# Attention in a latent-attention layer: probabilities times values by four query blocks, and where the rotary queries are made

## The chip, the cores and the metric

One NeuronCore of a Trainium2 chip runs the whole kernel. The metric is device time in microseconds (us) from launch to end. The engines work side by side, each through its own queue in order: TensorE (PE) multiplies matrices into PSUM, VectorE (DVE) and ScalarE (ACT) read PSUM and write SBUF, GpSimd (POOL) works on SBUF alone, and SyncE (SP) issues most of the DMAs.

## What is computed

One layer of a streaming encoder: 1024 tokens, width 1024, 16 heads (cut to what matters; `norm` is the RMS norm):

```python
u = norm(x, g) @ w_in                       # c_q 384 | c_kv 256 | k_rope 32 | z 1024
q = (norm(c_q) @ w_q_b)                     # per head 64 plain + 32 rotary columns
kv = norm(c_kv) @ w_kv_b                    # per head k_nope 64, v 64
q_rope, k_rope = rope(q[..., 64:]), rope(k_rope)
s = (q_nope @ k_nope.T + q_rope @ k_rope.T) * scale   # per block of 128 queries,
p = softmax(where(k_chunk <= q_chunk, s, -inf))       # keys up to the block's end, chunks of 64
x = x + (concat(p @ v) * silu(z)) @ w_out
x = x + sigmoid(norm(x) @ ple_gate) * (p_i @ ple_proj)
return norm(x, final_norm)
```

## The kernel before

All of it is in float32, in which each operand of a product is split into a high part, rounded to the PE's fast float32 form, and the low rest; a product is three matmuls (high times high, high times low, low times high). The program has five stages: u (the 672 columns of c_q, c_kv and k_rope, about 5 to 62 us of the trace), z (eight feature blocks `c`, to 161 us), attention (to about 507 us), the output projection, and the gate.

In **z**, each block `c` is 48 matmuls of 512 columns (L513). Its weights come in two halves through `z_weights`: SP loads `zs` (one buffer), ACT scales it to `zh` (L360), DVE makes the rest `zl` (L361); the halves are asked for two ahead. DVE scales the block on its way out of PSUM (L516).

**Rotary queries** are made by `project_r(g, hf)` for four heads `g` and one half `hf` of the tokens: nine matmuls of 512 columns (L423), two DVE products with the cosine and sine tables `cs` into the tile `rt` (L435), an ACT copy of the high part into `rh` (L438), a POOL subtraction that leaves the low part in `rt` (L91), and two POOL DMAs that write `rh` and `rt` to DRAM (L441), from where `rope_q` loads single heads. `rt` and `rh` have one buffer each, so a new `rt` can be written only when the DMA that reads the one before has landed. Before, two of the eight calls stand in z (blocks 4 and 5) and six among the heads 2, 6 and 10 of attention.

In **attention**, heads run one after the other, and in each head the eight blocks of 128 queries in the order of the list `ORDER`. For a block: scores on PE (`scores`, L609), maximum on DVE (L614), exponential on ACT (L619); two blocks later PE transposes the probabilities 128 by 128 (L121), ACT copies the high part of P^T (L650) and DVE the low part; when both blocks of a pair are there, `values` multiplies P^T by the values (L661), and o is evicted and multiplied with z. `project_k` makes the keys of two heads: DVE copies one head's rows to `kst` (L556) and makes `k_lo` of the other. Products take PSUM banks from a ring of four (`ps_pj`, `ps_o`, `ps_tr`), scores from two larger ones. A scheduler orders the instructions on each engine.

Line numbers are those of the kernel before, unless a fence says otherwise. The functions that the change touches follow.

Of the kernel before, what the change touches and what calls it, by code (L numbers as in the profile page):

```python
# [9 lines left out]
F32 = mybir.dt.float32  # L10
# [7 lines left out]
P = 128  # L18
S = 1024
# [17 lines left out]
ORDER = (5, 4, 2, 3, 7, 6, 0, 1)  # L37
# [3 lines left out]
V_AT, K_AT, Q_AT, R_AT = (4, 4, 2, 2), (0, 3), (6, 7), (1, 6)  # L41
# [10 lines left out]
def mla_ple_kernel(ctx, tc, x, x_t, p_t, pos, norm_g, w_c, w_z, q_norm, w_q, w_r, kv_norm, w_k, w_v,  # L52
# [9 lines left out]
    def pool(name, bufs=1, **kw):  # L62
        return tc.tile_pool(name=name, bufs=bufs, **kw)
# [327 lines left out]
    cs = [att1.tile([P, S], F32, name=f"cs{e}") for e in range(2)]  # L391
# [3 lines left out]
    def load_split(src, cols, name, bufs):  # L395
# [3 lines left out]
        hi = att1.tile([P, n], F32R, tag=name + "h", name=name + "h", bufs=bufs)  # L399
        lo = att1.tile([P, n], F32R, tag=name + "l", name=name + "l", bufs=bufs)  # L400
# [26 lines left out]
    def project_r(g, hf):  # L427
# [4 lines left out]
        ps = product_q(wr_of[g], hf)  # L432
# [68 lines left out]
    zw = zph.enter_context(pool("zw", reuse_waits="tile"))  # L501

    for c in range(KT):
# [20 lines left out]
        if c == 3:  # L524
            weights(0)
        if c in (4, 5):
            project_r(0, c - 4)
# [8 lines left out]
    pt_w = [[att.tile([P, n, 2 * P], F32R, name=f"pt{n}{z}") for z in "hl"] for n in (4, 8)]  # L536
    for n, w in zip((4, 8), pt_w):
        for z in w:
            G.memset(z[:, n - 1, :P].bitcast(F32), 0.0)
    pt = [[z[:, (2, 0, 2, 0)[g]:, :] for z in pt_w[g // 2]] for g in range(4)]  # L540
    vals = att.tile([P, NT, 2, 4, VD], F32R, name="vals")
    kst = att.tile([P, S], F32, name="kst")
# [4 lines left out]
    def project_k(c, hf):  # L547
# [93 lines left out]
    def prob_transposes(h, i, pr):  # L641
        g = i // 2
        hi, lo = pt[g]
        half = slice(0, P) if i % 2 == 0 else slice(P, 2 * P)
        for j0 in range(0, i + 1, 4):
# [4 lines left out]
            A.copy(out=hi[:, j0:j0 + n, half], in_=src)  # L650
            sub_hi(V, lo[:, j0:j0 + n, half], src, hi[:, j0:j0 + n, half])

    def values(h, g):
        e, c = h % 2, h // 2
        hi, lo = pt[g]
        ps = ps_o()
        last = 2 * g + 1
# [5 lines left out]
        o = att.tile([P, 256], F32, tag="o1", name="o1", bufs=2)  # L663
        A.copy(out=o[top], in_=ps[bot, :256])
        V.tensor_tensor(out=o[top], in0=ps[top, :256], in1=o[top], op=ALU.add)  # L665
        z = zT[top, c, g * 256:(g + 1) * 256]
# [18 lines left out]
    for n in range(len(blocks) + LAGV):  # L685
        if n < len(blocks):
# [209 lines left out]
```

## Time and profile before

| | us |
|---|---|
| median of three runs (719.19 to 720.9) | 719.9 |
| the profiled execution | 719.65 |
| its span, first to last instruction | 717.9 |
| PE busy in the span | 703.2 (98%) |
| DVE, ACT, POOL busy | 523.8, 400.5, 214.2 |

Matmuls overlap in this trace: a record lasts longer than the distance to the next one's start. What PE can do is read from distances of starts, not from durations. The profiled execution took 719.65 us, 1.75 us more than its span, for launch and end.

### The profile page before, as it was taken

To read this page: it belongs to the slowest core of one execution; us is meant where nothing else is said; L and a number is where in the kernel's file an instruction comes from. 1 tells how busy PE (TensorE), PEld (TensorE's weight loads), DVE (VectorE), ACT (ScalarE), POOL (GpSimd) and SP (SyncE) were. 2 spreads that over 40 slices of the span, in tenths; PEclk is the share of its full clock that TensorE was granted. 3 is DMA by queue.
4 is the path that set the end of the run, shared out by engine and by line. 5 is a ranking of instruction groups with operands and counts; after the bars stand their busy time and mean duration, and the time that the engine had idled before them with its cause. 6 is when DMAs were issued, how large, how long until landed. Compare 5 with 4: busy or idle time off the path is not lost.

```text
span 717.9 us, 11582 instructions
## 1 busy us (share of the span) xinstructions
PE 703.2 (98%) x4032; PEld 612.9 (85%) x4032; DVE 523.8 (73%) x1298; ACT 400.5 (56%) x920; POOL 214.2 (30%) x236
## 2 busy tenths in 40 slices
PE   9999999999999999999999999989999999999995
PEld 7999888888988899889988899878878888888884
DVE  6995553417888888888888888899564168888754
ACT  6752343417777767877767787776353145342322
POOL 0000443214145434554335532264155142000000
PEclk9999999999999999999999999999999999999999
DMA  8720334314103402052211421032573030111101
GB/s 318 279 89 12 122 100 125 103 60 110 38 16 108 147 31 74 1 181 74 66 40 60 136 60 60 15 108 85 179 265 115 1 102 24 38 37 37 60 30 59
DMA packets 26907, 63.95 MB, mean 89 GB/s; under 512 B 4568, under 2 KB 8544, under 8 KB 26848
## 3 DMA queue, kind: packets, MB, share of 16 engines
q1 hardware_dynamic: 23168, 52.19, 22.8%
q0 software_dynamic: 3536, 11.02, 4.6%
q8 instruction: 32, 0.52, 0.3%
q14 instruction: 27, 0.22, 0.1%
q10 hardware_dynamic: 144, 0.00, 0.0%
HBM read 50.01 MB, written 13.18 MB: 88 GB/s over the span
## 4 chain that ended last, share of the span: by engine, by line
PE 90%; DVE 3%; ACT 3%; DMA 2%; issue 1%; POOL 0%; SPq 0%; ACTq 0%; DVEq 0%
PE ps_big L751 21%; PE ps_big L609 13%; PE ps_big L513 12%; PE ps_o L661 10%; PE ps_tr L121 9%; PE ps_pj L423 6%; PE ps_big L215 4%; PE ps_pj L751 3%; PE ps_pj L570 3%; PE ps_pj L553 3%; PE ps_big L216 3%; PE ps_o L215 1%; PE ps_pj L216 1%; DMA wst<-in_w_out 1%; ACT prob L619 1%; PE ps_tr L609 1%
## 5 line engine op out<-in xcount | busy, mean ns | idle before, releaser
L751 PE MATMUL ps_big<-w,aTh 128*128 128x512 f32 (+1 forms) x480 | 139.0, 390 | 0.0
L751 PEld LDWEIGHTS ps_big<-w,aTh 128*128 128x128 f32 x480 | 89.4, 188 | 20.2
L619 ACT ACTIVATE prob<-ps_big,mx 128x384 f32<-128x384 f32 (+6 forms) x112 | 89.4, 798 | 16.2 <-DVE mx L614 15.5
L614 DVE TENSOR_REDUCE mx<-ps_big 128x1 f32<-128x384 f32 (+6 forms) x112 | 91.6, 818 | 1.8
L121 PE MATMUL ps_tr<-ident,prob 128*128 128x128 f32 x576 | 84.1, 273 | 2.0 <-ACT prob L619 2.0
L751 PE MATMUL ps_big<-w,aTl 128*128 128x512 f32 (+1 forms) x240 | 84.6, 390 | 0.0
L121 PEld LDWEIGHTS ps_tr<-ident,prob 128*128 128x128 f32 x576 | 68.3, 140 | 11.7 <-ACT prob L619 2.8
L91 DVE TENSOR_TENSOR pt8l<-ps_tr,pt8h 128x512 fp32r<-128x512 f32 (+3 forms) x128 | 71.0, 582 | 4.5 <-ACT pt8h L650 3.8
L667 POOL TENSOR_TENSOR zT<-o,zT 64x256 f32<-64x256 f32 x56 | 41.1, 736 | 94.2 <-DVE o L665 80.6
L609 PE MATMUL ps_big<-k_hi,qh 128*128 128x512 f32 (+2 forms) x176 | 67.7, 385 | 0.9 <-ACT prob L619 0.8
L650 ACT CAST pt8h<-ps_tr 128x512 fp32r<-128x512 f32 (+3 forms) x128 | 60.7, 509 | 4.7 <-PE ps_tr L121 4.3
L609 PE MATMUL ps_big<-k_lo,qh 128*128 128x512 f32 (+2 forms) x176 | 62.0, 352 | 0.0
L609 PE MATMUL ps_big<-k_hi,ql 128*128 128x512 f32 (+2 forms) x176 | 61.4, 349 | 0.0
L661 PE MATMUL ps_o<-pt8h,vals 128*128 128x256 f32 x224 | 57.6, 294 | 0.0
L661 PE MATMUL ps_o<-pt8l,vals 128*128 128x256 f32 x224 | 55.0, 282 | 0.0
L751 PEld LDWEIGHTS ps_big<-w,aTl 128*128 128x128 f32 x240 | 45.0, 188 | 10.2 <-POOL aTl L91 0.5
L116 ACT ACTIVATE jk<-xs 128x512 bf16<-128x512 f32 (+2 forms) x25 | 18.8, 751 | 45.2 <-DVE xs L829 37.3
L661 PEld LDWEIGHTS ps_o<-pt8l,vals 128*128 128x128 f32 x224 | 42.9, 191 | 0.0
L661 PEld LDWEIGHTS ps_o<-pt8h,vals 128*128 128x128 f32 x224 | 42.6, 190 | 0.0
L650 ACT CAST pt4h<-ps_tr 128x384 fp32r<-128x384 f32 (+3 forms) x64 | 27.2, 426 | 27.3 <-PE ps_tr L121 27.1
L360 ACT ACTIVATE zh<-zs,g_col 128x128 fp32r<-128x128 f32 x56 | 18.3, 392 | 42.1 <-DMA zs<-in_w_z 36.1
L609 PEld LDWEIGHTS ps_big<-k_hi,qh 128*128 128x128 f32 x176 | 33.2, 189 | 7.7 <-ACT prob L619 3.5
(285 smaller groups left out, 1740.2 us busy)
## 6 DMA issues: line engine op xcount, KB each, us to landing
zT<-in_x SPq DMA_DIRECT2D x8, 512.0 KB, 5.0
rlb<-rl SPq DMA_DIRECT2D x32, 128.0 KB, 3.1
wst<-in_w_out SPq DMA_DIRECT2D x8, 512.0 KB, 4.4
xs<-in_x SPq DMA_DIRECT2D x8, 512.0 KB, 7.2
wst<-in_ple_gate SPq DMA_DIRECT2D x8, 512.0 KB, 4.0
out<-xs SPq DMA_DIRECT2D x16, 256.0 KB, 2.0
zs<-in_w_z SPq DMA_DIRECT2D x14, 256.0 KB, 2.9
zT<-in_x_t SPq DMA_DIRECT2D x6, 512.0 KB, 4.1
```

The costliest lines, as they stand in the source:

```text
L91: eng.tensor_tensor(out=lo, in0=src, in1=hi.bitcast(F32), op=ALU.subtract)
L121: nc.tensor.transpose(dst[:, j * P:(j + 1) * P], src[:, j * P:(j + 1) * P], ident)
L215: nc.tensor.matmul(pq, st, mv[:, k, :QL], start=first, stop=last)
L423: nc.tensor.matmul(ps, w[b][:, k, :], (cq_hi, cq_lo)[a][:, k, hf * 512:hf * 512 + 512], start=k == 0 and a + b == 0, stop=k == n - 1 and a ...
L513: nc.tensor.matmul(ps[:, hf * 512:(hf + 1) * 512], wz[b][:, k % 4, :], (hT_hi, hT_lo)[a][:, k, hf * 512:(hf + 1) * 512], start=k == 0 and ...
L609: nc.tensor.matmul(ps[:, off + s0:off + s1], q[a][:, qs], (k_hi, k_lo)[b][e][:, s0:s1], start=a + b == 0, stop=a == 1)
L614: V.tensor_reduce(out=mx, in_=s, axis=AX.X, op=ALU.max, negate=True)
L619: A.activation(out=pr[:, :n], in_=s, func=AF.Exp, bias=mx, scale=1.0, accum_out=l)
L650: A.copy(out=hi[:, j0:j0 + n, half], in_=src)
L661: nc.tensor.matmul(ps[:, :256], w, z[:, j, :], start=j + n == 0, stop=j == last and n == 1)
L667: (V if h >= H - 2 else G).tensor_tensor(out=z, in0=o[top], in1=z, op=ALU.mult)
L751: nc.tensor.matmul(o, st[a][:, k, :], w[k][b][:, cols], start=k == 0 and a + b == 0, stop=k == nk - 1 and a == 1)
```

## The change

1. `ORDER` becomes (5, 4, 1, 0, 7, 6, 3, 2). `values` runs for four query blocks at once (`g = i // 4`): up to 512 columns in one matmul. P^T is packed: below the diagonal four blocks side by side, on the diagonal four, three, two and one (10 blocks of 128 columns in all), so the diagonal's matmuls have 512, 384, 256 and 128 columns. Each diagonal group of four transposes is copied in two parts (three and one). The evictions of o have 512 columns instead of 256.
2. All eight `project_r` calls stand in z: two after each of the blocks 4 to 7, with their weights (`weights_r`) loaded one group ahead; `cs` moves to a pool that ends with z. None is left in attention.
3. `kst`, a tile of its own before, is now the tile `rt`.
4. `rsqrt` makes its first guess in one DVE instruction instead of two, and its Newton step with one column uses `scalar_tensor_tensor` in place of `tensor_scalar`.
5. The last token block's final scaling goes out in four pieces of 256 columns (two on ACT, two on DVE), one of them through ACT's own DMA queue.

```diff
-ORDER = (5, 4, 2, 3, 7, 6, 0, 1)
+ORDER = (5, 4, 1, 0, 7, 6, 3, 2)
...
-        half = small.tile([P, n], I32, tag=f"rs_i{n}", name="rs_i", bufs=2)
-        V.tensor_scalar(out=half, in0=v.bitcast(I32), scalar1=1, scalar2=None,
-                        op0=ALU.logical_shift_right)
-        V.tensor_scalar(out=y.bitcast(I32), in0=half, scalar1=-1, scalar2=0x5F3759DF,
+        V.tensor_scalar(out=y.bitcast(I32), in0=v.bitcast(I32), scalar1=-0.5, scalar2=0x5F3759DF,
...
-                V.tensor_scalar(out=t, in0=y, scalar1=y, scalar2=h, op0=ALU.mult, op1=ALU.mult)
+                V.scalar_tensor_tensor(out=t, in0=y, scalar=y, in1=h, op0=ALU.mult, op1=ALU.mult)
...
-        if c == 3:
-            weights(0)
-        if c in (4, 5):
-            project_r(0, c - 4)
+            wr = weights_r(0)
+        if c >= 4:
+            for hf in range(2):
+                project_r(c - 4, wr, hf)
+            if c + 1 < KT:
+                wr = weights_r(c - 3)
+            else:
+                weights(0)
...
-    kst = att.tile([P, S], F32, name="kst")
+    kst = {}
...
+        if hf == 0:
+            kst[0] = rt_tile("kst")
+        V.tensor_copy(out=kst[0][NOPE:, cols], in_=ps[NOPE:])
...
+            if j0 < 4 * g:
+                parts = [(slice(0, 4), slice(q, 16, 4))]
+            else:
+                m = min(n, 3)
+                parts = [(slice(0, m), slice(16 * g + q, 16 * g + q + 3 * m - 2, 3))]
+                if n == 4:
+                    parts.append((slice(3, 4), slice(16 * g + 7, 16 * g + 8)))
...
-        for j in range(last + 1):
-            w = vals[:, j, c % 2, 2 * e:2 * e + 2, :]
-            for n, z in enumerate((hi, lo)):
-                nc.tensor.matmul(ps[:, :256], w, z[:, j, :], start=j + n == 0, stop=j == last and n == 1)
+        steps = [(j, n) for j in range(4 * g + 4) for n in range(2)]
+        steps.append(steps.pop(1))
+        for j, n in steps:
+            q = max(j - 4 * g, 0)
+            at = 4 * j if j < 4 * g else 16 * g + (7 if q == 3 else 4 * q)
+            nc.tensor.matmul(ps[:, q * P:], vals[:, j, c % 2, 2 * e:2 * e + 2, :],
+                             pt[g][n][:, at:at + 4 - q, :], start=j + n == 0, stop=(j, n) == (0, 1))
...
-                if h % 4 == 2 and h + 2 < H and at in R_AT:
-                    project_r(h // 4 + 1, R_AT.index(at))
...
-        for hf in range(2):
-            cols = halves[hf]
-            if last and hf == 0:
+        for i, cols in enumerate([slice(z, z + 256) for z in range(0, D, 256)] if last else halves):
+            on_act = last and i < 2
+            if on_act:
```

Three places show what the scheduler makes of it. On DVE, the end of z and the start of attention before: `rt` is written by the last rotary product of z, then come the scaling of the last z blocks and the first keys and queries (a bracket lists what an instruction waits for: DMAHW and DMASW are DMAs of SP's and of POOL's queue).

```order
L435 TENSOR_TENSOR rt_1587<-ps_pj_1577,cs0_982 128x512 [waits DMASW5_49,PE_49,Pool_49]
L435 TENSOR_TENSOR rt_1587<-ps_pj_1577,cs1_983 128x512
...
L516 TENSOR_TENSOR zT_81<-ps_big_1595,rbc_994 128x1024 [waits PE_49]
L516 TENSOR_TENSOR zT_81<-ps_big_1670,rbc_994 128x1024 [waits PE_49]
L556 COPY kst_1736<-ps_pj_1750 64x512 [waits DVE_49,Activation_49]
L91 TENSOR_TENSOR k_lo0_988<-ps_pj_1750,k_hi0_987 64x512
```

The same place on DVE with the change:

```order
L515 TENSOR_TENSOR zT_81<-ps_big_1609,rbc_974 128x1024 [waits PE_49]
L429 TENSOR_TENSOR rt_1696<-ps_pj_1686,cs0_987 128x512 [waits DMASW3_49,PE_49,Pool_49]
L429 TENSOR_TENSOR rt_1696<-ps_pj_1686,cs1_988 128x512
L429 TENSOR_TENSOR rt_1714<-ps_pj_1704,cs0_987 128x512 [waits DMASW5_49,PE_49,Pool_49]
...
L515 TENSOR_TENSOR zT_81<-ps_big_1728,rbc_974 128x1024 [waits PE_49]
L429 TENSOR_TENSOR rt_1791<-ps_pj_1781,cs0_987 128x512 [waits DMASW7_49,PE_49,Pool_49]
...
L429 TENSOR_TENSOR rt_1809<-ps_pj_1799,cs0_987 128x512 [waits DMASW1_49,PE_49,Pool_49]
...
L557 COPY kst_1867<-ps_pj_1859 64x512 [waits DMASW3_49,Pool_49]
L91 TENSOR_TENSOR k_lo0_968<-ps_pj_1859,k_hi0_967 64x512
```

The last four rotary products (of eight, from block 4 on) stand here, each behind the landing of a POOL DMA, and the first copy to `kst`, ahead of every `k_lo`, waits for the last of them.

On SP with the change, the loads of the first heads' rotary queries stand behind the weights of a later head pair, whose staging buffer POOL has to free:

```order
L394 DMA ws_1908<-in_w_q 128x384 [waits DMAHW7_49,Pool_49]
L394 DMA ws_1914<-in_w_k 128x256 [waits DMAHW4_49,Pool_49]
L394 DMA ws_2382<-in_w_q 128x384 [waits DMAHW6_49,Pool_49]
L584 DMA qh_1847<-rq0h_1446 32x1024 [waits DMASW2_49,DMASW3_49,DMASW1_49,DMASW4_49,DMASW0_49,DMASW6_49,DVE_49,DMAHW1_49,PE_49,Activation_49]
L584 DMA qh_1847<-rq0h_1446 32x1024
```

What moved here: these loads had two rotary products ahead of them in the program and have eight now; `ws` has two buffers, and the last `ws` above reuses the one that POOL frees only after the last rotary product.

On PE, one `values` call before (blocks 0 and 1 of a head, 4 matmuls) and what stands around it:

```order
L609 MATMUL ps_big_2505<-k_hi0_987,qh_2249 128x512
L661 MATMUL ps_o_2480<-pt4h_1727,vals_1735 128x256
L661 MATMUL ps_o_2480<-pt4l_1728,vals_1735 128x256
...
L628 MATMUL ps_tr_2491<-ident_61,rl_2489 16x128
L609 MATMUL ps_big_2505<-k_lo0_988,qh_2249 128x512
```

and one with the change (blocks 0 to 3, 8 matmuls):

```order
L669 MATMUL ps_o_2262<-pt0h_1841,vals_1845 128x512
L669 MATMUL ps_o_2262<-pt0h_1841,vals_1845 128x384
L669 MATMUL ps_o_2262<-pt0l_1842,vals_1845 128x384
L669 MATMUL ps_o_2262<-pt0h_1841,vals_1845 128x256
L669 MATMUL ps_o_2262<-pt0l_1842,vals_1845 128x256
L669 MATMUL ps_o_2262<-pt0h_1841,vals_1845 128x128
L669 MATMUL ps_o_2262<-pt0l_1842,vals_1845 128x128
L669 MATMUL ps_o_2262<-pt0l_1842,vals_1845 128x512
```

A head had 4 + 8 + 12 + 16 = 40 matmuls of 256 columns; it has 8 + 16 = 24 now, twelve of 512 columns and four each of 384, 256 and 128.

## Rows read from the trace of the kernel before

**Rows 1.** Busy us of each engine in two stretches, granted clock (PEclk), DMA.

```profile
core 0: us, PE busy (x) PEld busy (x) DVE busy (x) ACT busy (x) POOL busy (x), PEclk, DMA share, GB/s
480.00:500.00 20.00, 16.63 (x114) 14.55 (x114) 18.94 (x37) 13.17 (x33) 12.37 (x8) 1.00 0.35 100
...
180.00:460.00 280.00, 280.00 (x1888) 254.06 (x1887) 241.28 (x518) 209.65 (x503) 114.85 (x122) 1.00 0.23 70
```

**Rows 2.** Timeline of PE in attention: start us, duration us, instruction.

```profile
300.95 0.28 PE L661 MATMUL ps_o<-pt8l,vals 128*128 128x256 f32 x1
301.07 0.34 PE L609 MATMUL ps_big<-k_hi,qh 128*128 128x384 f32 x1
301.25 0.34 PE L609 MATMUL ps_big<-k_lo,qh 128*128 128x384 f32 x1
...
301.60 0.82 PE L121 MATMUL ps_tr<-ident,prob 128*128 128x128 f32 x6
302.17 0.48 PE L609 MATMUL ps_big<-k_hi,qh 128*128 128x512 f32 x1
302.49 0.40 PE L609 MATMUL ps_big<-k_lo,qh 128*128 128x512 f32 x1
```

**Rows 3.** Timeline of DVE in z: how blocks 3, 4 and 5 leave PSUM.

```profile
113.80 1.22 DVE L516 TENSOR_TENSOR zT<-ps_big,rbc 128x1024 f32<-128x1024 f32 x1 [0.23 <-PE ps_big L513]
...
124.68 1.23 DVE L516 TENSOR_TENSOR zT<-ps_big,rbc 128x1024 f32<-128x1024 f32 x1 [2.33 <-PE ps_big L513]
...
137.68 1.23 DVE L516 TENSOR_TENSOR zT<-ps_big,rbc 128x1024 f32<-128x1024 f32 x1 [3.73 <-PE ps_big L513]
```

**Rows 4.** Timeline of the first rotary product's way through DVE, ACT and POOL.

```profile
126.88 1.28 DVE L435 TENSOR_TENSOR rt<-ps_pj,cs 128x512 f32<-128x512 f32 x2
128.19 1.05 ACT L438 CAST rh<-rt 128x1024 fp32r<-128x1024 f32 x1 [0.73 <-DVE rt L435]
129.33 2.40 POOL L91 TENSOR_TENSOR rt<-rt,rh 128x1024 fp32r<-128x1024 f32 x1 [12.54 <-ACT rh L438]
...
132.43 0.74 POOL L441 DMA_DIRECT2D rq0l<-rt  x1
```

**Rows 5.** By tile: landing of the eight DMAs that read `rt`, then `rh`.

```profile
DMA to landing us min/median/max: 4.0/4.6/6.1
...
DMA to landing us min/median/max: 3.2/3.3/4.6
```

**Rows 6.** Timeline of the start of attention.

```profile
161.36 0.40 PE L553 MATMUL ps_pj<-ckv_hi,wkh 128*128 128x512 f32 x1
...
167.08 0.69 DVE L556 COPY kst<-ps_pj 64x512 f32<-64x512 f32 x1
...
167.81 0.68 DVE L91 TENSOR_TENSOR k_lo<-ps_pj,k_hi 64x512 fp32r<-64x512 f32 x1
```

**Rows 7.** PE's first matmuls of the program (timeline).

```profile
1.23 3.66 PE L153 MATMUL ps_tr<-zT 128*128 128x512 bf16 x9 [1.23 <-DVE zT L150]
```

**Rows 8.** DVE's groups by shape: busy us, mean ns, idle before.

```profile
L91 DVE TENSOR_TENSOR pt8l<-ps_tr,pt8h 128x512 fp32r<-128x512 f32 x80 | 53.3, 681 | 3.1 <-ACT pt8h L650 2.7
L665 DVE TENSOR_TENSOR o<-ps_o,o 64x256 f32<-64x256 f32 x64 | 26.8, 419 | 6.3 <-ACT o L664 5.4
L91 DVE TENSOR_TENSOR ql<-ps_pj,qh 64x512 fp32r<-64x512 f32 x32 | 22.0, 689 | 11.1 <-ACT qh L592 9.7
...
L91 DVE TENSOR_TENSOR pt8l<-ps_tr,pt8h 128x384 fp32r<-128x384 f32 x16 | 8.8, 553 | 1.2 <-ACT pt8h L650 1.2
...
L91 DVE TENSOR_TENSOR pt8l<-ps_tr,pt8h 128x128 fp32r<-128x128 f32 x16 | 4.4, 278 | 0.0
```

**Rows 9.** Timeline of the last block's inverse root and scaling.

```profile
711.15 0.15 DVE L96 TENSOR_SCALAR rs_i<-ms 128x1 int32<-128x1 int32 x1
...
711.53 0.27 DVE L106 TENSOR_SCALAR rs_t<-r,rs_h 128x1 f32<-128x1 f32 x1
711.83 0.16 DVE L107 SCALAR_TENSOR_TENSOR r<-rs_t,r 128x1 f32<-128x1 f32 x1
712.03 0.27 DVE L106 TENSOR_SCALAR rs_t<-r,rs_h 128x1 f32<-128x1 f32 x1
...
713.10 0.72 ACT L841 ACTIVATE xs<-xs,r 128x512 f32<-128x512 f32 x1 [2.17 <-DVE r L107]
```

More of the change, by code (lines that the diff above doesn't have):

```diff
@@ L390, in mla_ple_kernel, with load_split @@
     att1 = late.enter_context(pool("att1", side="right"))
-    cs = [att1.tile([P, S], F32, name=f"cs{e}") for e in range(2)]
     att2 = late.enter_context(pool("att2", side="right"))
     k_hi, k_lo = zip(*([att2.tile([P, S], F32R, name=f"k_{z}{e}") for z in ("hi", "lo")] for e in range(2)))
-    def load_split(src, cols, name, bufs):
+    def load_split(src, cols, name, bufs, home=att1):
         n = math.prod(cols)
@@ L501, in mla_ple_kernel, with weights_r @@
     zw = zph.enter_context(pool("zw", reuse_waits="tile"))
+    cs = [zw.tile([P, S], F32, name=f"cs{e}") for e in range(2)]
+    def weights_r(g):
+        return load_split(w_r[g], (QL // P, P), "wr", 1, zw)
     for c in range(KT):
@@ L533, in mla_ple_kernel @@
     att = atts.enter_context(pool("att"))
[L536 to L540, printed above, removed]
+    pt = [[att.tile([P, 16 * g + 10, P], F32R, name=f"pt{g}{z}") for z in "hl"] for g in range(2)]
     vals = att.tile([P, NT, 2, 4, VD], F32R, name="vals")
-    kst = att.tile([P, S], F32, name="kst")
+    kst = {}
     def prob_tile():
@@ L555, in project_k @@
         A.copy(out=k_hi[0][:NOPE, cols], in_=ps[:NOPE])
-        V.tensor_copy(out=kst[NOPE:, cols], in_=ps[NOPE:])
+        if hf == 0:
+            kst[0] = rt_tile("kst")
+        V.tensor_copy(out=kst[0][NOPE:, cols], in_=ps[NOPE:])
         sub_hi(V, k_lo[0][:NOPE, cols], ps[:NOPE], k_hi[0][:NOPE, cols])
     def odd_k():
-        A.copy(out=k_hi[1][NOPE:], in_=kst[NOPE:])
-        sub_hi(G, k_lo[1][NOPE:], kst[NOPE:], k_hi[1][NOPE:])
+        A.copy(out=k_hi[1][NOPE:], in_=kst[0][NOPE:])
+        sub_hi(G, k_lo[1][NOPE:], kst[0][NOPE:], k_hi[1][NOPE:])
     def project_v(g, t):
@@ L649, in prob_transposes @@
             src = tr[:, :n * P].rearrange("p (k n) -> p k n", n=P)
-            A.copy(out=hi[:, j0:j0 + n, half], in_=src)
-            sub_hi(V, lo[:, j0:j0 + n, half], src, hi[:, j0:j0 + n, half])
+            if j0 < 4 * g:
[5 more added lines that the diff above has]
+                    parts.append((slice(3, 4), slice(16 * g + 7, 16 * g + 8)))
+            for ks, to in parts:
+                hi, lo = (z[:, to, :] for z in pt[g])
+                A.copy(out=hi, in_=src[:, ks])
+                sub_hi(V, lo, src[:, ks], hi)
     def values(h, g):
         e, c = h % 2, h // 2
-        hi, lo = pt[g]
         ps = ps_o()
-        last = 2 * g + 1
-        for j in range(last + 1):
-            w = vals[:, j, c % 2, 2 * e:2 * e + 2, :]
-            for n, z in enumerate((hi, lo)):
-                nc.tensor.matmul(ps[:, :256], w, z[:, j, :], start=j + n == 0, stop=j == last and n == 1)
+        steps = [(j, n) for j in range(4 * g + 4) for n in range(2)]
[5 more added lines that the diff above has]
+                             pt[g][n][:, at:at + 4 - q, :], start=j + n == 0, stop=(j, n) == (0, 1))
         top, bot = slice(e * VD, (e + 1) * VD), slice((1 - e) * VD, (2 - e) * VD)
[L663 to L666, printed above, removed]
+        o = att.tile([P, 512], F32, tag="o1", name="o1", bufs=2)
+        A.copy(out=o[top], in_=ps[bot])
+        V.tensor_tensor(out=o[top], in0=ps[top], in1=o[top], op=ALU.add)
+        z = zT[top, c, g * 512:(g + 1) * 512]
         (V if h >= H - 2 else G).tensor_tensor(out=z, in0=o[top], in1=z, op=ALU.mult)
@@ L708, in mla_ple_kernel @@
             prob_transposes(*blocks[n - LAG], probs.pop(n - LAG))
-        if n >= LAGV and (blocks[n - LAGV][1] ^ 1) in order(blocks[n - LAGV][0])[:(n - LAGV) % NT]:
-            h, i = blocks[n - LAGV]
-            values(h, i // 2)
+        h, i = blocks[n - LAGV]
+        g = i // 4
+        if n >= LAGV and i == [z for z in order(h) if z // 4 == g][-1]:
+            values(h, g)
             if h % 2 and i == order(h)[-1] and n < len(blocks):
@@ L844, in mla_ple_kernel @@
                                        in1=f_bc[:, cols], op0=ALU.mult, op1=ALU.mult)
-            nc.sync.dma_start(out=out[t * P:(t + 1) * P, cols], in_=xs[:, t, cols])
+            (nc.scalar if on_act and i else nc.sync).dma_start(out=out[t * P:(t + 1) * P, cols], in_=xs[:, t, cols])
 def kernel(**inputs):
```

18 lines of the change are left out of this document (7 added, 11 removed).

## Prediction

> **What bounds the kernel now.** I first read the busy time by stretches. From 180 to 460 us PE is busy for all of 280.00 us, at a granted clock of 1.00, while DVE has 241.28, ACT 209.65 and POOL 114.85 [rows 1]. A busy PE may still be waiting inside its records, since they overlap, so I went on to the timeline and took distances between starts. A 256-column matmul is followed after 0.12 us, a 384-column one after 0.18. Six transposes and one 512-column matmul take from 301.60 to 302.49; with 0.23 for the latter a transpose costs 0.11 [rows 2]. In z one block of 48 matmuls takes 124.68 - 113.80 = 10.88 us, 0.227 each [rows 3]. These distances stand back to back in attention and in z: the kernel is a row of matmuls without holes, and a change is worth what it takes from the row or what hole it tears. The one stretch with holes is the end of attention: PE is busy for 16.63 us of 20 from 480 to 500, with DVE at 18.94 [rows 1].
>
> **Values in groups of four.** Before: 40 matmuls of 0.12 in a head, 4.80 us. After: twelve of 512 columns at 0.23, four of 384 at 0.18, four of 256 at 0.12 and four of 128 columns at a price x that no row here shows: 2.76 + 0.72 + 0.48 + 4x = 3.96 + 4x. If half the columns cost half as much, x is 0.06 and a head saves 0.60 us; if a short matmul in this number form is slower per column and costs what 512 columns do, x is 0.23 and a head loses 0.08. The transposes also move 128 columns, though not in that form, and cost 0.11 [rows 2]; I take x = 0.12, the 256-column price, as nearest to it. Then 16 heads save 16 x 0.36 = **5.8 us** (bounds: 9.6 saved, 1.3 lost).
>
> The evictions do not eat this. On DVE a split copy is 553 + 278 ns instead of 681, twice a head: 0.30 us more. The evictions of o are two of 689 (64 by 512) instead of four of 419: 0.30 less [rows 8]. DVE also loses six rotary products of 1.28 us [rows 4] to z. So DVE stays near its 86% [rows 1], and I count nothing; the cover is that slack, and without it each 0.1 us a head would cost 1.6.
>
> **All rotary queries in z.** For PE the work only moves: a rotary product is 13.00 - 10.88 = 2.12 us [rows 3], and six of them go from attention to z, 12.7 us there and back. The rest of the product is the point. The tile `rt` has one buffer, and the next product may write it only after the DMA from it has landed. One pass, from the first DVE multiplication at 126.88 over ACT at 128.19 and POOL at 129.33 to the issue of the DMA at 132.43, is 5.55 us [rows 4]; the landing adds 4.0 to 6.1, in the median 4.6 [rows 5]. A link of the chain is thus 10.2 us (9.6 to 11.7). Before, links were apart by a z block or by blocks of attention and nobody waited. After, eight stand in a row behind each other, from 126.88 on, since nothing ahead of block 4 moves: the multiplications start at 126.9, 137.1, ... and 198.3, and the last DMA lands at 126.88 + 8 x 10.2 = 208.5. PE is through long before: it would begin the first keys at 161.36 + 12.7 = 174.1 [rows 6].
>
> Who waits for the chain's end? `kst` is the tile `rt` now, so DVE's first copy of it waits for the eighth landing, and the order puts it ahead of every `k_lo`, without which no score is complete. Two copies and two `k_lo` of 0.69 and 0.68 us follow [rows 6]: keys are complete at 208.5 + 2.7 = 211.2. Before, this was at 167.81 + 0.68 = 168.5, that is 7.1 us after the first keys' matmul; shifted by the moved work, 181.2. So attention is late by 30.0 us. PE can use some of it: two products of values stand ahead, 12 matmuls of 0.12, 1.5 us. **28.5 us** of hole remain; as a formula, eight links minus 53.1.
>
> PE gets there in steps. Its four PSUM banks are given back by the multiplications: the first queries wait for the sixth (to 179.2), the next keys for the seventh (189.4), the next queries for the eighth (199.6), each a link apart. z itself is not held up: DVE also makes `zl` between the links, but the last of it stands between the third and the fourth multiplication, ahead of PE's need. SP's loads of the rotary queries stand behind a weight load that waits for POOL after the last link, at 204.6 or later; keys are not complete by then, so I give them no term.
>
> After the hole PE has to start again behind new scores, maxima and exponentials, and perhaps with a slower clock. Nine warm-up matmuls of 512 columns at the program's start take 3.66 us, 0.41 each [rows 7], against 0.23: that is the pace of 1.2 GHz. The Trainium skill (TensorE: Matmul & The Clock Gate, What's actually happening) says that an idle TensorE falls back to half its clock and gets it back only by sustained work; no row of this kernel shows a fall in mid-program, since it has no such hole. I take 2.5 us for the restart (0 to 5).
>
> **The rest.** The shorter inverse root is behind other work wherever PE is busy; at the very end nothing covers it. There it saves one instruction of 0.15 and three times 0.27 - 0.16: **0.5 us** [rows 9]. The last scaling in four pieces of 256 columns still takes ACT about the 0.72 of one piece of 512 [rows 9]; a smaller last DMA may save some tenths, which I leave at nothing. In the last two heads the larger value products come in an already torn stretch [rows 1]; two us either way, taken as nothing.
>
> **Sum.** 719.65 (the profiled execution: 717.9 of span and 1.75 around it, 0.25 under the median of 719.9) + 28.5 + 2.5 - 5.8 - 0.5 = **744 us**.
>
> **Rivals.**
>
> *The chain is hidden.* Then only the gains count: 719.65 - 5.8 - 0.5 = 713 us, faster. It needs a link of at most 53.1 / 8 = 6.6 us, and the sign turns where the hole and its restart are worth the 6.3 us gained, at a link of 7.1. For it: z and its eight products last until 174 and POOL is idle most of that time. Against it: 5.55 us of the link are executed instructions, which leaves 1.1 to 1.6 for a landing of which the fastest took 4.0 [rows 4, 5].
>
> *Shorter links.* The DMAs from `rh`, issued just ahead, land in 3.3 us in the median [rows 5]. If those from `rt` did too, a link would be 8.9, the hole 17.7 and the time 734. The Trainium skill (DMA: Bandwidth & Descriptors, Anatomy of one DMA) gives 2.0 us plus the bytes at 436 GB/s, for the 512 KB here 3.2: an estimate of 733 us. The trace has 4.0 to 6.1 for all eight from `rt`, so the rule fits those from `rh` and not these.
>
> *Dearer.* If x is 0.23, 7.1 us are added: 751. If all landings take 6.1, the links are 11.7 and the hole 40: 756. Both together are unlikely.
>
> *It does nothing measurable.* A hole of just about 4 us would be needed, for which no row speaks.
>
> **How the numbers follow.** My forecast's case (737 to 750) has 6 in 10: the chain is in the order and every link has been executed before. Shorter links (732 to 737) have 13 in 100, the dearer cases (750 to 758) 17, the hidden chain 8, the rest 2. The range from 732 to 758 takes in all the slower cases and leaves out the hidden chain and the tails. Within 0.2% is about what a measurement of this kernel can tell from no change; faster by more has 8 in 100, within it 1, slower 91.
>
> **What would show it.** In the trace after: eight multiplications into `rt` about 10 us apart, over 80 us; PE without matmuls for some 3, 8, 9 and 7 us between 175 and 211; the first `kst` copy released by a DMA at about 208; 24 value matmuls a head, whose 128-column ones tell x by the distance to the next start. I am wrong if links are under 7 us, if `kst` does not wait, or if value products or evictions make PE wait inside attention, which now has lumps of up to 16 matmuls (3.3 us) in a row.

## The result and the profile after

The changed kernel takes **774.7 us** in the median of four runs (772.39 to 776.15), the kernel before 719.6 beside it: a ratio of 1.0763, with a 95% interval from 1.073 to 1.0796. I had forecast 744 and a range up to 758. The sign was right, the size was not: 55.2 us lost instead of 24. The profiled execution took 774.66 us, with a span of 772.9.

The hole ahead of the first scores came as forecast. The view by tile of `rt` in the changed kernel (least, median and greatest duration in ns, first and last start) has the chain, and its last line the landings that answer to [rows 5]:

```profile
L429 DVE TENSOR_TENSOR rt<-ps_pj,cs x16: 679/681/693, 127.5 to 198.4; 128x512 f32<-128x512 f32 x16
...
DMA to landing us min/median/max: 4.0/4.1/6.5
```

Two multiplications to a product: the eighth product's begin at 197.8 us; I had put it at 198.3. The timeline of PE after shows where PE stood until a multiplication gave a bank back, and at last until a `k_lo` came:

```profile
179.56 0.80 PE L417 MATMUL ps_pj<-cq_hi,wqh 128*128 128x512 f32 x1 [3.45 <-DVE rt L429]
189.22 0.80 PE L552 MATMUL ps_pj<-ckv_hi,wkh 128*128 128x512 f32 x1 [5.99 <-DVE rt L429]
199.10 0.79 PE L417 MATMUL ps_pj<-cq_hi,wqh 128*128 128x512 f32 x1 [6.95 <-DVE rt L429]
...
211.30 0.79 PE L610 MATMUL ps_big<-k_lo,qh 128*128 128x512 f32 x1 [3.51 <-DVE k_lo L91]
```

The starts were forecast at 179.2, 189.4 and 199.6, the complete keys at 211.2. The timeline of DVE after, which answers to [rows 6], has `kst` released by the landing and the last `k_lo` done at 212.7:

```profile
209.85 0.69 DVE L557 COPY kst<-ps_pj 64x512 f32<-64x512 f32 x1 [3.09 <-DMA rq3l<-rt]
...
212.00 0.68 DVE L91 TENSOR_TENSOR k_lo<-ps_pj,k_hi 64x512 fp32r<-64x512 f32 x1
```

What was not forecast lies behind it. The busy times by stretches of the changed kernel; the last row is the stretch of [rows 1] in which PE was busy throughout before:

```profile
core 0: us, PE busy (x) PEld busy (x) DVE busy (x) ACT busy (x) POOL busy (x), PEclk, DMA share, GB/s
160.00:180.00 20.00, 16.55 (x72) 13.35 (x71) 4.38 (x7) 3.58 (x4) 11.30 (x11) 0.98 0.39 135
180.00:200.00 20.00, 7.06 (x17) 4.80 (x17) 3.21 (x5) 6.13 (x8) 8.65 (x8) 0.67 0.32 115
200.00:220.00 20.00, 14.61 (x70) 12.34 (x70) 9.97 (x20) 7.99 (x18) 7.64 (x6) 0.76 0.46 138
180.00:460.00 280.00, 247.62 (x1413) 211.42 (x1413) 205.36 (x445) 183.50 (x438) 86.89 (x77) 0.94 0.20 58
```

PE lacks 18.3 us between 180 and 220, but 32.4 between 180 and 460. So some 14 us of PE's idle time lie inside attention, behind the hole. To place them, read from each timeline when a head's first score begins. The starts below, in us from the span's start, are those of single profiled executions; all kernels but the first two are experiments of the next section.

| kernel | first keys | head 1 | head 4 | head 8 | head 12 | head 15 | last value product's last matmul | span |
|---|---|---|---|---|---|---|---|---|
| before | 161.4 | 185.1 | 251.1 | 336.8 | 422.5 | 485.5 | 507.5 | 717.9 |
| changed | 174.6 | 229.0 | 294.8 | 383.7 | 472.5 | 536.2 | 561.9 | 772.9 |
| rotary queries in z alone | 174.4 | 228.2 | 291.6 | 375.1 | 458.6 | 521.5 | 543.6 | 753.9 |
| changed, order of before | 175.1 | 228.7 | 293.2 | 378.2 | 463.2 | 526.7 | 553.1 | 764.1 |
| without rotary products in attention | 162.3 | 186.0 | 250.1 | 333.6 | 417.2 | 480.0 | 502.2 | 711.9 |
| without 4 of 40 value matmuls | 162.6 | 186.2 | 251.9 | 337.4 | 422.9 | 486.7 | 508.2 | 718.7 |
| rotary alone, two tiles, spread | 174.5 | 205.4 | 269.3 | 352.8 | 436.3 | 499.2 | 521.4 | 732.4 |

Head 1 starts 43.9 us late; the prediction's terms make 12.7 + 28.5 + 2.5 = 43.7 (that they meet so closely is partly luck, see the account below). From there the forecast was 19.0 us shorter than before (12.7, 5.8 and 0.5). In fact the rest is 11.1 us longer (55.0 between the spans, less 43.9). **The whole miss of 30 us lies behind the first scores.** Four heads, 4 to 7, take 88.9 us; before they took 85.7.

The waits of PE after, from 294 to 545 us (us in total, times, longest):

```profile
PE ps_big L610 <- ACT prob L620: 11.0, 9, 2.1
PE ps_tr L118 <- DVE pt1l L91: 2.6, 6, 0.6
```

and those of its weight loads:

```profile
PEld ps_big L610 <- ACT prob L620: 15.1, 13, 2.4
PEld ps_tr L118 <- PE ps_tr L118: 3.9, 6, 0.8
```

The two lists overlap: the wait shown next stands in the first with 2.12 us and in the second with 2.42, so their sums may not be added. A score cannot start until the exponentials have freed one of the two tiles `ps_big`. One such wait in the timeline of all engines after, at the head's blocks 7, 6 and 3:

```profile
262.85 0.58 ACT L673 COPY o<-ps_o 64x512 f32<-64x512 f32 x1 [0.94 <-PE ps_o L669]
...
263.46 0.69 DVE L674 TENSOR_TENSOR o<-ps_o,o 64x512 f32<-64x512 f32 x1 [0.17 <-ACT o L673]
...
264.19 1.22 DVE L615 TENSOR_REDUCE mx<-ps_big 128x1 f32<-128x1024 f32 x1
...
264.38 0.27 PE L118 MATMUL ps_tr<-ident,prob 128*128 128x128 f32 x1
...
265.51 1.11 ACT L620 ACTIVATE prob<-ps_big,mx 128x1024 f32<-128x1024 f32 x1 [0.56 <-DVE mx L615]
...
266.77 0.50 PE L610 MATMUL ps_big<-k_hi,qh 128*128 128x512 f32 x1 [2.12 <-ACT prob L620]
```

DVE evicts `o`, takes block 7's maximum, ACT makes its exponentials, and only then PE has a tile for the next scores. In the meantime it had one transpose to do, since the blocks whose probabilities were due, 1 and 0, are the two smallest.

### The profile page after: what moved, and what is told of

It is laid out like the page before. It is cut to its first block, busy times and chain, and to the rows that moved or that the text cites. A ratio compares the mean times of both kernels' runs of the same rounds, so it can differ in the third digit from the quotient of the medians.

```text
span 772.9 us, 10984 instructions
## 1 busy us (share of the span) xinstructions
PE 717.7 (93%) x3776; PEld 607.2 (79%) x3776; DVE 518.8 (67%) x1270; ACT 402.0 (52%) x921; POOL 208.2 (27%) x204
## 5 line engine op out<-in xcount | busy, mean ns | idle before, releaser
L620 ACT ACTIVATE prob<-ps_big,mx 128x896 f32<-128x896 f32 (+6 forms) x112 | 89.3, 798 | 20.7 <-DVE mx L615 19.1
L615 DVE TENSOR_REDUCE mx<-ps_big 128x1 f32<-128x896 f32 (+6 forms) x112 | 91.0, 813 | 1.5
L91 DVE TENSOR_TENSOR pt1l<-ps_tr,pt1h 128x128 fp32r<-128x128 f32 (+2 forms) x144 | 74.1, 537 | 12.6 <-ACT pt1h L658 10.3
L676 POOL TENSOR_TENSOR zT<-o,zT 64x512 f32<-64x512 f32 x28 | 36.0, 1284 | 144.7 <-DVE o L674 144.6
L658 ACT CAST pt1h<-ps_tr 128x128 fp32r<-128x128 f32 (+3 forms) x144 | 63.4, 469 | 12.5 <-PE ps_tr L118 11.3
L669 PE MATMUL ps_o<-pt1h,vals 128*128 128x512 f32 (+3 forms) x128 | 42.9, 361 | 0.0
L669 PE MATMUL ps_o<-pt1l,vals 128*128 128x512 f32 (+3 forms) x128 | 41.6, 364 | 0.0
L658 ACT CAST pt0h<-ps_tr 128x384 fp32r<-128x384 f32 (+2 forms) x80 | 29.2, 372 | 23.3 <-PE ps_tr L118 18.1
L610 PEld LDWEIGHTS ps_big<-k_lo,qh 128*128 128x128 f32 x176 | 34.3, 195 | 6.0 <-DVE k_lo L91 3.7
L357 ACT ACTIVATE zh<-zs,g_col 128x128 fp32r<-128x128 f32 x56 | 18.3, 392 | 38.8 <-DMA zs<-in_w_z 30.3
L429 DVE TENSOR_TENSOR rt<-ps_pj,cs 128x512 f32<-128x512 f32 x16 | 10.3, 685 | 41.7 <-DMA rq2l<-rt 15.6
```

The source lines that it names most:

```text
L91: eng.tensor_tensor(out=lo, in0=src, in1=hi.bitcast(F32), op=ALU.subtract)
L357: A.activation(out=hi[:, k, :], in_=stg[:, k, :], func=AF.Copy, scale=g)
L429: V.tensor_tensor(out=t[:, n, :], in0=ps, in1=cs[n][:, cols], op=ALU.mult)
L610: nc.tensor.matmul(ps[:, off + s0:off + s1], q[a][:, qs], (k_hi, k_lo)[b][e][:, s0:s1], start=a + b == 0, stop=a == 1)
L615: V.tensor_reduce(out=mx, in_=s, axis=AX.X, op=ALU.max, negate=True)
L620: A.activation(out=pr[:, :n], in_=s, func=AF.Exp, bias=mx, scale=1.0, accum_out=l)
```

## The experiments

**Rotary queries in z alone.** The kernel before with all rotary queries made during z and `kst` as the tile `rt`, and nothing else of the change; its core:

```diff
+            for hf in range(2):
+                project_r(c - 4, wr, hf)
...
-                if h % 4 == 2 and h + 2 < H and at in R_AT:
-                    project_r(h // 4 + 1, R_AT.index(at))
...
+            kst[0] = rt_tile("kst")
```

> The kernel before with one part of the change alone: all eight rotary products in z, with kst as the tile rt; values stay in groups of two. Theory A (the hole of 31 us before the first scores is all that this part costs, the work itself only moves from attention to z): 719.7 + 31 = 751 us, attention from the first score of head 1 to the output projection shorter than before by 12.7 us. Theory B (heads 2, 6 and 10 are set by DVE and ACT once the products have left them, so that little comes back): up to 763 us, attention shorter by 0 to 6 us. Keys complete at about 212 in both.

Measured: 756.1 us (ratio 1.0511, 1.0483 to 1.0538), between the two. Head 1 is 43.1 us late, the end 36.1: attention gives back 7.0 of the 12.7 us that left it. Heads 4 to 7 (stretches of the trace, columns as above):

```profile
291.58:375.05 83.47, 82.25 (x561) 74.49 (x559) 71.46 (x155) 62.44 (x154) 28.71 (x33) 1.00 0.17 50
```

They take 2.2 us less than before, though 4.2 us of matmuls left them. And everything else in the change, which I had priced at -6.3, costs 774.7 - 756.1 = 18.6 us.

**A second tile for every other product.** On the changed kernel, paid for with a buffer of z's weights:

```diff
-                           for z, d, m in (("s", F32, 1), ("h", F32R, 3), ("l", F32R, 3)))
+                           for z, d, m in (("s", F32, 1), ("h", F32R, 2), ("l", F32R, 2)))
...
-        t = rt_tile("rt").rearrange("p (c n) -> p c n", c=2)
+        t = (zw.tile([P, S], F32, tag="rtz", name="rtz", bufs=1) if hf == 0 else rt_tile("rt")).rearrange("p (c n) -> p c n", c=2)
```

> The changed kernel with a second tile for every other rotary product, paid for by a buffer less for each half of z's weights. If the single buffer rt is what holds up the first scores: the hole of 31 us shrinks to 0 to 6 and the time is 744 to 750 us; the clock stays at 1.00 up to attention. Rival (the chain is held by POOL, the DMA queue or z itself): keys complete near 212 as in the changed kernel, 772 to 777 us. In both, the part of the loss that lies inside attention stays.

Measured: 766.5 us, 8 less; neither expectation was met. Two rows of its timeline tell why:

```profile
155.80 1.05 ACT L432 CAST rh<-rt 128x1024 fp32r<-128x1024 f32 x1 [5.72 <-DMA rq1h<-rh]
...
202.10 0.69 DVE L557 COPY kst<-ps_pj 64x512 f32<-64x512 f32 x1 [5.34 <-DMA rq3l<-rt]
```

With `rt` doubled, the single `rh` is next: ACT's cast waits for the DMA that reads it. Two products follow each other at 6.8 us instead of 9.7 to 9.9, and since the last pair stands behind z, `kst` is only 7.8 us earlier.

**The products spread over z**, with the second tile, on the kernel with pairs; eight places in z from the middle of its fifth block on:

```diff
+R_AT = (35, 38, 42, 45, 49, 52, 56, 59)
...
+            if 8 * c + k in R_AT:
+                r = R_AT.index(8 * c + k)
+                project_r(r // 2, wr, r % 2)
...
```

> The kernel before with all rotary products in z (values in groups of two), a second tile for every other product, and the eight products spread over z from the middle of its fifth block to the middle of its eighth. The last DMA of the chain should land at about 180 instead of 209 us, and the hole ahead of the first scores should shrink from 31 to about 4 us. What is left tells what it is worth to move 12.7 us of rotary products out of attention. Theory A (the work only moves): 721 to 724 us. Theory B (attention gives back 7 of 12.7 us, as the kernel with rotary queries in z showed from head 1 on): 727 to 730 us. Rival (the hole is held by something else): 745 us or more.

Measured: 735.9 us (1.0233, 1.0214 to 1.0251), 20 less than with one tile at the end of each block. With a shorter chain that ends earlier most of the hole goes, so the chain is its cause; the second tile and the spreading were not timed apart. The first `kst` in its timeline of DVE:

```profile
183.94 0.69 DVE L565 COPY kst<-ps_pj 64x512 f32<-64x512 f32 x1 [8.06 <-DMA rq3l<-rt]
```

My numbers were too low: head 1 is late by 20.4 us, 12.7 of moved work and 7.7 of hole instead of 4; and the end by 14.5, so attention gives back 5.9 of 12.7.

**What the rotary products were worth in attention.** The kernel before without them, no work moved:

```diff
-        for z, d in zip(q_of[h], rq_of[h // 4]):
+        for z, d in zip(q_of[h], rq_of[0]):
...
-                if h % 4 == 2 and h + 2 < H and at in R_AT:
-                    project_r(h // 4 + 1, R_AT.index(at))
```

> The kernel before without the six rotary products that lie in attention (heads 4 to 15 take the rotary queries of the first group, so their scores are not the reference's). It prices what the change takes out of attention. My prediction's step says 12.7 us less (707 us). Theory B (heads 2, 6 and 10 have DVE and ACT as their next bound, so the products filled time that PE would have waited) says 6 to 8 us less: 711.5 to 713.5 us.

Measured: 715.3 us, 4.0 less (ratio 0.9945, 0.9928 to 0.9962, or 2.7 to 5.2 us). That is under even theory B. Heads 4 to 7:

```profile
250.06:333.64 83.58, 82.36 (x561) 74.49 (x560) 71.52 (x155) 62.41 (x154) 30.19 (x35) 1.00 0.18 52
```

With 4.2 us of matmuls gone the stretch is 2.1 us shorter and PE has 1.2 us without work, where it had none.

**What value matmuls are worth in attention.** The kernel before without 4 of the 40 of a head:

```diff
-                nc.tensor.matmul(ps[:, :256], w, z[:, j, :], start=j + n == 0, stop=j == last and n == 1)
+                if j or not n:
+                    nc.tensor.matmul(ps[:, :256], w, z[:, j, :], start=j + n == 0, stop=j == last and n == 1)
```

> The kernel before without four of the 40 value matmuls of a head (the first low half of each pair of blocks, so the output lacks those terms): 64 matmuls of 0.12 us, 7.7 us of PE's work, a little more than the 6.6 us by which groups of four shorten it; DVE, ACT and POOL do what they did. My prediction's step, that a microsecond off PE's row is a microsecond of time, says 712 us. Theory B (attention gives back a third, as with the rotary products left out: 4.0 of 12.7) says 716.5 to 718 us.

Measured: 719.9 us, ratio 1.001 (0.9993 to 1.0027): **7.7 us of PE's work taken away, and nothing comes back.** Even theory B was too hopeful. The granted clock of its profiled execution stays at 1.00 up to 485 us, and from head 4 to head 12, where 3.8 us of matmuls left, it takes 171.0 us instead of 171.4. Heads 4 to 7:

```profile
251.92:337.41 85.49, 84.72 (x562) 75.58 (x561) 73.42 (x159) 63.85 (x155) 37.79 (x41) 1.00 0.25 76
```

and PE's weight loads in the same stretch wait more often, in small pieces, for what comes round from ACT and DVE (0.4, 0.4 and 0.2 us in these three before):

```profile
PEld ps_big L609 <- ACT prob L619: 1.2, 4, 0.6
PEld ps_tr L121 <- issue: 0.9, 3, 0.3
PEld ps_o L662 <- DVE pt8l L91: 0.8, 2, 0.6
```

**Where value products stand.** First by the order of the blocks, which leaves P^T free for longer:

```diff
-ORDER = (5, 4, 1, 0, 7, 6, 3, 2)
+ORDER = (5, 4, 7, 6, 1, 0, 3, 2)
```

> The changed kernel with the order of the query blocks 5, 4, 7, 6, 1, 0, 3, 2, so that the two value products of a head come four blocks apart instead of two and the tiles of P^T are free two blocks earlier. Theory C (bunched value products and the tight reuse of P^T cost the 28 us that attention loses): 748 to 762 us, with fewer gaps of over 0.5 us before the scores. Theory B (the loss is that of heads that DVE and ACT set): 772 to 777 us. The hole of 31 us is the same in both.

Measured: 773.4 us. Theory C falls. Attention from head 1 on is 4 us shorter, but head 1 starts 3 us later. Then with each product in two halves a block apart, in two orders. At each change to the next four heads, new values are written between the halves of the last products, so these sums are not the reference's; the instructions are the same:

```diff
+        for s, (j, n) in enumerate(steps):
+            if s == len(steps) // 2:
+                yield
```

> The changed kernel with each value product issued in two halves, the second one block of scores later. Before this run: value products in fours cost 18.6 us over the kernel that has only the rotary queries in z (774.7 against 756.1), where I had forecast a gain of 5.8. Theory D1 (lumps of 8 and 16 matmuls hold PE between two halves of one block's scores, so that maxima and exponentials come late): shorter lumps give back 6 to 15 us, 760 to 769 us. Theory D2 (ACT and DVE stand in their queues at the eviction of o until the lump has ended): little changes, since they still stand there, 772 to 777. Theory D3 (the evictions of P^T cost ACT and DVE more): 773 to 777.

> Both halves of the value products apart and the order 5, 4, 7, 6, 1, 0, 3, 2. Theory D1: the best of the kernels with value products in fours and one tile rt, 755 to 766 us, two to four under the one with halves alone. Theory D3: 771 to 775 us, as with the order alone (773.4).

Measured: 771.2 and 776.8 us. The first lies between what D1 and D2 asked for, the second above both of its forecasts. Then with `o` evicted one block later:

```diff
                              pt[g][n][:, at:at + 4 - q, :], start=j + n == 0, stop=(j, n) == (0, 1))
+        yield
```

> The changed kernel with the eviction of o (ACT's copy, DVE's sum, POOL's product) issued one block of scores after its value product. Theory D2: ACT and DVE find the product ended and no longer stand before o (13.8 and 8.8 us between 294 and 545 us in the changed kernel); 760 to 769 us. Theory D1 or D3: 772 to 777 us.

Measured: 769.8 us, 5 less, at the edge of what D2 asked for: a part, not the cause. Nor need the 5 us be the eviction's own: three falls of the clock inside attention are gone as well, for which the last section estimates 5 us. Last in pieces of four matmuls, which needs a bank of its own for `o`, with a control:

```diff
-        return psum.tile([P, 512], F32, tag="one", name="ps_tr", bufs=4)
+        return psum.tile([P, 512], F32, tag="one", name="ps_tr", bufs=3)
...
-        return psum.tile([P, 512], F32, tag="one", name="ps_o", bufs=4)
+        return psum.tile([P, 512], F32, tag="o", name="ps_o", bufs=1)
...
```

> The changed kernel with a PSUM bank for o of its own, and three in turn for transposes and projections instead of four for all three: a control for the next run. No theory asks for a difference: 772 to 777 us; with one bank less for the transposes up to 5 us more.

> The changed kernel with o in a bank of its own and each value product in pieces of four matmuls, one piece after the scores of a block, in six blocks of eight; the order of the blocks is 5, 4, 7, 6, 1, 0, 3, 2. No lump on PE is longer than four matmuls. Theory D1 (lumps of 8 and 16 matmuls leave ACT and DVE without scores, and afterwards PE waits for them): attention falls back to about that of the kernel with pairs, 752 to 762 us. If lumps are not the cause: 770 to 778 us.

Measured: 785.3 for the control, 10.6 above the changed kernel, more than any theory had asked for: giving `o` one bank of its own and leaving three for the rest is dear. In pieces 788.1, 2.8 above a control that lacks the order of blocks of the pieces (alone, that order was worth 1.3 us). So **lumps do not look like the cause**: D1 falls, as far as three banks in turn allow to say.

**The order of the blocks.** I had not priced that line of the change at all. Alone on the kernel with pairs, then undone on the changed kernel, then a third order:

```diff
-ORDER = (5, 4, 1, 0, 7, 6, 3, 2)
+ORDER = (5, 4, 2, 3, 7, 6, 0, 1)
```

> The kernel with all rotary queries in z and values in groups of two (756.1 us), with one line of the change more: the order of the query blocks 5, 4, 1, 0, 7, 6, 3, 2 instead of 5, 4, 2, 3, 7, 6, 0, 1. Theory E (the order is what costs: blocks 7 and 6 come right behind the two smallest, so PE fills both score buffers and has only three transposes to do until the exponentials of block 7 free one): 764 to 772 us. Rival F (the grouping by four itself costs, by the time that a product holds its bank and P^T): 754 to 758 us.

> The changed kernel with the order of the query blocks of before, 5, 4, 2, 3, 7, 6, 0, 1; values stay in groups of four. Theory E: 757 to 767 us. Rival F: 772 to 777 us.

> The changed kernel with 7, 6, 3, 2, 5, 4, 1, 0 in every head, the order that the last head has already: two blocks of middle size stand between the largest pairs, and the value products of 16 and 8 matmuls fall behind blocks 6 and 2. Theory E: 757 to 770 us, PE's waits before scores (26 us between 294 and 545 us in the changed kernel) at most half. Rival F: 772 to 780 us.

Measured: with pairs a ratio of 1.0513 (1.0493 to 1.0533, some 757 us), the same as the 1.0511 without it; with fours 764.4 us (1.0608, 1.0591 to 1.0626), 10.3 less than the changed kernel; the third order 771.9. So with the order of before theory E holds for the changed kernel, and rival F for pairs: order and grouping cost only together. The waits of PE with the order of before, from 284 to 535 us:

```profile
PE ps_big L610 <- ACT prob L620: 4.7, 7, 0.9
PE ps_tr L118 <- ACT prob L620: 3.2, 4, 1.6
```

and of its weight loads:

```profile
PEld ps_big L610 <- ACT prob L620: 6.3, 7, 1.1
PEld ps_tr L118 <- ACT prob L620: 5.3, 10, 1.8
```

Before scores PE waits 4.7 us instead of 11.0 and its loads 6.3 instead of 15.1, in stretches of 251 us that begin 10 us apart. But these waits are not the measure of the loss. With the third order they are as short, and theory E's time (757 to 770 us) is missed all the same; PE waits elsewhere, from 284 to 535 us:

```profile
PE ps_pj L417 <- DVE pt1l L91: 7.8, 6, 1.3
PE ps_big L610 <- ACT prob L620: 3.9, 5, 1.5
```

**The last head's order**, on the changed kernel with the order of before:

```diff
-LAST = (7, 6, 3, 2, 5, 4, 1, 0)
+LAST = (7, 6, 5, 4, 3, 2, 1, 0)
```

> The changed kernel with the order of before (764.4 us) and, in the last head, 7, 6, 5, 4, 3, 2, 1, 0, so that its product of 16 matmuls comes before its last scores are through. If the two lumps behind the last scores are what the end loses against pairs (4.3 us between the first scores of head 15 and the last value product): 760 to 762 us. If not: 763 to 766 us.

Measured: 763.5 us (1.0617, 1.0587 to 1.0647), no difference that can be told from 764.4. From head 15's first score to the last value matmul it takes 26.6 us, as before the edit (26.4), against 22.1 with pairs. This loss stays unexplained; with the order of before the granted clock is 0.50 from 525.5 to 528.5 us, which I estimate at 1.5 us of it at most.

**All repairs together**: two tiles and spread products, order of before, new last order, `o` evicted later, each as shown.

> The changed kernel with everything that gave something back: the rotary products spread over z with a second tile (20 us with pairs), the order of before (10), the last head's order (0 to 4) and the later eviction of o (0 to 5). Sum: 734 to 745 us. Theory F (groups of four gain nothing once order and hole are mended, since PE's time is not what attention lacks): 736 us or more, not under the same kernel with pairs (735.9). If groups of four are worth their 5.8 us: 730 us.

Measured: 740.3 us (1.0287, 1.027 to 1.0304), 4.4 above the same hole's repair with pairs. That is as theory F has it: groups of four gain nothing even so.

**The end alone.** The kernel before with the shorter inverse root and the last scaling in four pieces, timed twice:

```diff
-        half = small.tile([P, n], I32, tag=f"rs_i{n}", name="rs_i", bufs=2)
...
+        for i, cols in enumerate([slice(z, z + 256) for z in range(0, D, 256)] if last else halves):
```

> The kernel before with the shorter inverse root and the last scaling in four pieces alone: 0.5 us less than before, 719.1 us, no more than 0.2% either way. Rival (the shorter root also speeds up normalisation in attention, or the smaller last DMA counts): 717 us or less.

> The kernel before with the shorter inverse root and the last scaling in four pieces, timed in more rounds: 0.5 to 1.1 us under before, 718.6 to 719.2 us. It is the only part of the change that was not slower; this settles whether it is faster.

Measured: 718.6 and 718.5 us, ratios of 0.9988 (0.9974 to 1.0003) and 0.9989 (0.9979 to 0.9999). It is the one version here with the reference's result that beats both kernels, by 0.8 us (0.1 to 1.5) in the second timing; the interval of the first still takes in no change.

## Why the prediction was wrong

Its terms, and what the runs put in their places (us):

| step | forecast | measured | from |
|---|---|---|---|
| moved work, hole and restart up to head 1 | +43.7 | +43.9 | starts of head 1 |
| rotary products leave attention | -12.7 | -7.0 | rotary queries in z alone; 4.0 (2.7 to 5.2) where they are only left out |
| values in groups of four, with their order | -5.8 | +19.4 | 18.6 between two kernels, and 0.8 that the end gains |
| end | -0.5 | -0.8 | the end alone |

They make +55.5, against 55.2 between the medians; the rows come from different executions.

**The hole: right, step by step.** A link of 10.2 us (measured 9.7 to 10.8), a bank given back with each, `kst` behind the eighth landing. Keys were complete at 212.7 us instead of 211.2. That the sum came out within 0.2 us is partly luck: against these 1.5 us PE did four products of values ahead of the last wait, 24 matmuls or 2.8 us, where I had counted two and 1.5. PE stood for 3.5, 6.0, 7.0 and 3.5 us, not for 3, 8, 9 and 7, in part since it worked between the waits at half clock. That it is the chain and not z is shown by the kernels with two tiles: less chain, less hole (8 and 20 us). The restart: behind each of its four waits PE ran at a granted clock of 0.50, which is 1.2 GHz; what that cost by itself was not measured. The stretches of the changed kernel, the second one at the beginning of a wait:

```profile
179.50:182.00 2.50, 2.44 (x6) 1.96 (x7) 1.14 (x2) 2.35 (x3) 1.28 (x1) 0.50 0.00 0
183.00:185.50 2.50, 0.23 (x1) 0.00 (x0) 0.00 (x0) 0.70 (x3) 1.50 (x3) 1.00 0.47 180
186.50:192.00 5.50, 2.78 (x6) 1.82 (x6) 1.29 (x2) 1.04 (x1) 1.62 (x1) 0.50 0.13 51
197.00:202.00 5.00, 2.90 (x7) 2.32 (x8) 1.97 (x3) 2.10 (x3) 1.75 (x1) 0.50 0.48 134
211.50:216.00 4.50, 4.50 (x19) 4.31 (x20) 2.77 (x7) 1.28 (x2) 2.36 (x1) 0.50 0.00 0
```

The Trainium skill (TensorE: Matmul & The Clock Gate, What's actually happening) says that an idle TensorE falls back to half its clock; this trace agrees, 0.50 behind each hole.

**"The kernel is a row of matmuls without holes, and a change is worth what it takes from the row": this step failed**, and two terms with it. The rows were read rightly [rows 1, 2]: PE had no wait to speak of. But that nobody waits on PE's row does not say that the next bound is far below. Four value matmuls a head, 7.7 us, taken out give nothing (at most 0.5 by the interval); the six rotary products, 12.7 us, give 4.0. No engine is full next: in the kernel without the four matmuls DVE is busy for 73.4 of 85.5 us, 86%, and ACT for 75%. What I take to be the bound is the round that a block makes, from scores to maximum to exponentials, which frees one of two tiles for the next scores. PE's new waits are at those places, but no run gave attention a third score tile, so that the round is the bound was not shown.

**"For PE the work only moves"** is the same error: of 12.7 us that leave heads 2, 6 and 10, between 4 and 7 come back. As I read it, the products were work that PE did while the round went on.

**"Then 16 heads save 16 x 0.36."** The price x that I had to guess was even better than taken: in the trace after, a 128-column matmul is followed by its partner after 0.062 us and by the 512-column one after 0.111 (medians of 32 distances in value products; I took 0.12). A head's value products take 4.3 us by the medians for each number of columns, against 40 times 0.12 before the grouping: PE's row is 7 to 8 us shorter over 16 heads, and none of it arrives. What is lost instead: 10 us by the order of the blocks, in groups of four only; 4.3 us in the last head (26.4 instead of 22.1 us); 4.6 us between heads 1 and 15 at the old order (late by 0.5 and 5.1 us against the kernel with pairs). The first is shown as the price of that line, though not by which wait it arises: the falls of the clock that go with it may be up to half. The last two are placed but not explained; 5 us of the total come back when `o` is evicted later. The last head is also the term that I had taken as nothing, "two us either way": it was +3.8 in the changed kernel (25.75 us against 21.93 before).

**"I count nothing; the cover is that slack."** As a load this was right: heads 4 to 7 have 70.86 us of DVE and 62.71 of ACT after, 71.46 and 62.44 with pairs. Evictions cost nothing by their busy time. That they cost by standing in front of a maximum is how I read the wait shown above; the kernel with the later eviction of `o` doesn't prove it, since its clock changed too.

**Nothing for SP's loads, half a microsecond for the end:** right for the loads, since at 211.30 PE waits for `k_lo`, not for queries. For the end the 0.5 us lies within the measured 0.1 to 1.5, but not by its parts. The inverse root at the very end after, which answers to [rows 9]:

```profile
766.49 0.15 DVE L96 TENSOR_SCALAR r<-ms 128x1 int32<-128x1 int32 x1
...
766.74 0.22 DVE L103 SCALAR_TENSOR_TENSOR rs_t<-r,rs_h 128x1 f32<-128x1 f32 x1
...
768.14 0.91 ACT L849 ACTIVATE xs<-xs,r 128x256 f32<-128x256 f32 x2 [1.88 <-DVE r L104]
```

From the shift to ACT it is 1.65 us instead of 1.95; an iteration's first step is 0.22 instead of 0.27, not 0.16 as I had it, while the two pieces on ACT take 0.91 instead of 0.72. These parts make 0.1 us; whether the smaller last DMA gave the rest, no run shows.

What I named as a sign of being wrong, value products that make PE wait inside attention, came true, but with no price and no chance in the sum.

## What to carry to other kernels

An engine that is busy throughout may have another bound right beneath it: before a saving is counted, leave a little of its work out and time it. Here 7.7 us left out gave nothing, and a run of that kind would have moved the forecast more than any reading of rows. When a change regroups work, price the new order as an edit of its own: the same order cost 10 us with large groups and nothing with small ones. And a chain through a single buffer is computed well from its link (here within 1.5 us after 85), but doubling one buffer hands the chain to the next single one.

## What the hardware showed beside

- Matmuls of 128 columns in this number form follow each other at 0.062 us where the weights stay and at 0.111 where the next brings new ones; the 256-column price of 0.12 is no floor.
- A bank of PSUM can be worth more than it looks: one bank for `o` alone and three in turn for transposes and projections, instead of four for all, cost 10.6 us. Which of the two halves costs was not timed apart.
- The clock also falls inside attention. In the changed kernel three waits of 2.1 us before a score (up to 266.8, 355.7 and 444.5 us) are each followed by a granted clock of 0.50, at which transposes follow each other at 0.213 us instead of 0.109. From head 1 to the last value product, in the changed kernel, the one with `o` evicted later and the one with the blocks in the order 5, 4, 7, 6, 1, 0, 3, 2:

```profile
340.00:360.00 20.00, 17.21 (x99) 15.05 (x97) 15.40 (x35) 14.14 (x35) 8.12 (x7) 0.91 0.13 34
229.00:561.90 332.90, 311.41 (x1836) 267.20 (x1836) 266.32 (x580) 234.49 (x570) 106.70 (x87) 0.98 0.17 49
...
230.10:557.20 327.10, 307.36 (x1837) 263.01 (x1836) 266.06 (x581) 233.29 (x570) 107.04 (x87) 1.00 0.18 50
...
232.00:560.10 328.10, 305.94 (x1821) 260.58 (x1820) 260.39 (x575) 229.52 (x565) 106.49 (x87) 1.00 0.17 49
```

  The first row is one of the three stretches with a fall; the other two (260 to 280 and 440 to 460 us) have 0.91 too. Three times 20 us at 0.91 are an estimate of 5 us of PE's time, and the two kernels without falls are 5.8 and 4.8 us shorter here. So long waits may cost twice, once by themselves and once by the clock behind them; no run separates the two.
